# Attention scores from hi and lo parts, and a first modulation with eight tiles

## The chip, the cores and the metric

The kernel runs on one core of a Trainium2 chip. The metric is device time in microseconds (us) for one execution, the median of several. TensorE (PE) multiplies, with weight loads shown as PEld; VectorE (DVE), ScalarE (ACT) and GpSimd (POOL) work elementwise; transfers between HBM and the core's memory are handed out by the queues of SyncE (SP), ScalarE and GpSimd and run on 16 shared DMA engines. Each engine runs its instructions in order.

## The reference

Two layers of a transformer over 256 image tokens x and 256 context tokens, width 1024. In each layer both streams are modulated by rows made of `silu(c) @ w_ada + b_ada`, projected by `w_in` (queries, keys, values, convolution input, gates), mixed by a differential attention and a convolution of 31 taps, and sent through a mixture of 16 experts. In the second layer only x is carried on. The part that the change touches:

```python
hx = modulate(x, mod_x[0], mod_x[1])          # x * (1 + scale) + shift
px = hx @ w_in_l
qx = apply_rope(qk_heads(px[..., :Q_END]), cos, sin)      # 4 heads, 2 maps of 64
s = jnp.einsum('bqhmd,bkhmd->bhmqk', q, k) * (DA_HEAD_DIM ** -0.5)
a = jax.nn.softmax(s, axis=-1)
a = a[:, :, 0] - lam * a[:, :, 1]
return jnp.einsum('bhqk,bkhe->bqhe', a, v)
```

All data is fp32.

## The kernel before

**Products in parts.** The large products of a mixer run in fp32r, a form of fp32 with fewer bits that TensorE takes in one pass. Each operand is split into a hi part (ScalarE casts it to fp32r, L286) and a lo part (the rest, one subtraction, L287), and `mm3` adds three products, hi x hi (L317), hi x lo (L320) and lo x hi (L321), in one bank. `split_unit` does this for a raw weight tile of 128x2048 in two halves; the engine that subtracts is an argument, VectorE by default. The parts lie in rings `whi` and `wlo` of four tiles each. Raw weight tiles lie in `raw`, a ring of three (1 MB each); `load_raw` takes the next one and issues the load on SP's queue (L270). Smaller products run on fp32 data directly, TensorE making several passes; the profile shows such a product as two records.

**The start.** x and ctx are loaded by ScalarE's queue and transposed on TensorE into `xT` (eight blocks, tiles m1a and m1b). `ada(0, 0, "mm")` makes the first modulation: eight raw tiles of `w_ada`, each with four fp32 products of 32 rows (L377), a row out of the bank (L382), transposes, and `modT` (L390, L391). A tile pool named `start` is closed behind it, so the mixer's pool reuses its memory.

**The mixer** (one for each layer). In the first layer `first_block(0)` loads the weights of the first projection block (two raw tiles, 1024x512) and splits them with GpSimd as the subtracting engine; then `modulate` makes, for each of eight k, `hh` on ScalarE (L515) and, on VectorE, the full product (L516) and `hl` (L519). Blocks of projections follow, each 96 products of 512 columns for both streams: two of the convolution, queries, keys, values, and six more for gates. In the second layer the first block is split by VectorE at the end of the layer before.

Queries and keys come out with tokens as rows. On the tiles of x `rope` turns them on VectorE (L621 to L626; its swapped copy `sw` is a "qt" tile), others are copied; TensorE transposes them into the only bank "tr", and ScalarE copies the bank into `kT` (L647) and, scaled, into `qT` (L649), both fp32.

**Attention.** For each tile of 128 queries, four heads and two maps, one score product (L665) of 64 rows, with the two maps in the upper and lower half of TensorE's rows, 512 keys wide for x and 256 for ctx (first layer only). VectorE takes the maximum (L670), ScalarE the exponential (L672), VectorE joins the two maps, TensorE transposes, and the product with the values follows (L686). Between them `pace` and notes of order (`follow`) spread the gates' products and the convolution's taps (L719, L721 on VectorE), so that TensorE has other work while a head's chain runs. The tile's output goes through `o` (a "qt" tile) into hi and lo parts `ah` and `al` (L708).

**End of the convolution.** Four channel blocks: ScalarE and VectorE make z and t (L768 to L770, "zt" tiles, a ring of two) and split z into `ch` and `cl`.

Tiles of one name are a ring: "qt" has three, "at" six (exponentials and transposed maps), "zt" two. The order of instructions within each engine is made when the kernel is built, by a planner that goes by priority in program order and by its own costs and due times.

Of the kernel before, what the change touches and what calls it, by code (L numbers as in the profile page):

```python
# [25 lines left out]
F32 = mybir.dt.float32  # L26
F32R = mybir.dt.float32r
# [133 lines left out]
def dit_kernel(ctx: ExitStack, tc: tile.TileContext, A, out):  # L161
# [40 lines left out]

    ident = C("ident")

    crow = cst.tile([16, 128], F32, name="crow")
    S.dma_start(crow[0:8, :], A["c"].rearrange("o (k p) -> (o k) p", p=128))
    S.dma_start(crow[8:16, :], A["c_ctx"].rearrange("(k p) -> k p", p=128))

# [98 lines left out]
    def block_parts(rs, engs=(V, V)):  # L307

        res = []
        for raw in rs:  # L310
            for hi, lo in split_unit(raw, engs):
                for j in range(2):
                    res.append((hi[:, j * 512:(j + 1) * 512], lo[:, j * 512:(j + 1) * 512]))
        return res
# [24 lines left out]
    G.dma_start(wr[:, :, :NE], A["w_router"].rearrange("(k p) e -> p k e", p=128))  # L339
    br = cst.tile([128, NE], F32, name="br")  # L340
    G.dma_start(br, bcast_rows(A["b_router"]))

    start = scoped("start", tr=2, mm=1)
    st0 = start.open()


    cs = cst.tile([128, KC, 32], F32, name="cs")
# [142 lines left out]
        V.tensor_scalar(dst, r, mean, rs, op0=OP.subtract, op1=OP.mult)  # L490

    def first_block(l):
        return block_parts(block_raws(A["w_in"][l].rearrange("(k p) n -> p k n", p=128), U_OFF + CC, KC), (V, V) if l else (G, G))

    def mixer(l, src, gT, bT, fill, front=None, first=None):

# [79 lines left out]
        if front:  # L576
            front(0, pa, modulate)
        else:
            first = first_block(l)
            for k in range(KC):  # L580
                modulate(k, (0, 1), lambda s: src[k][:, 256 * s:256 * s + 256])

# [17 lines left out]
        if front:  # L600
            front(1, pa, modulate)

            ts = [pa.tile([128, 2, D], F32, name=name) for name in ("ah", "al")]
            for i, name in enumerate(("ln2_g", "ln2_b")):
                rows = xres[i * 128:i * 128 + 128, :]
                G.dma_start(ts[i][:, 0, :], rows)
                G.dma_start(ts[i][:, 1, :], bcast_rows(A[name][l - 1]))
            for i, t in enumerate(ts):
                V.tensor_tensor(t[:, 0, :], t[:, 0, :], ts[0][:, 1, :], op=OP.mult)
                V.tensor_tensor(t[:, 0, :], t[:, 0, :], ts[1][:, 1, :], op=OP.add)  # L610
                G.dma_start(xres[i * 128:i * 128 + 128, :], t[:, 0, :])


        def rope(dst, ps, tt):
            cs_ = C("cos").rearrange("p (t d) -> p t d", t=2)[:, tt, :]
            sn_ = C("sin").rearrange("p (t d) -> p t d", t=2)[:, tt, :].rearrange("p (i two) -> p i two", two=2)
            sw = pa.tile([128, 512], F32, name="qt", bufs=3)
            dv = dst.rearrange("p (h i two) -> p h i two", h=8, two=2)
            pv = ps.rearrange("p (h i two) -> p h i two", h=8, two=2)
            sv = sw.rearrange("p (h i two) -> p h i two", h=8, two=2)  # L620
            V.tensor_tensor(dst.rearrange("p (h d) -> p h d", h=8), ps.rearrange("p (h d) -> p h d", h=8),  # L621
                            cs_[:, None, :].to_broadcast([128, 8, 64]), op=OP.mult)
            for b in range(2):
                V.tensor_tensor(sv[:, :, :, b], pv[:, :, :, 1 - b],
                                sn_[:, None, :, b].to_broadcast([128, 8, 32]), op=OP.mult)
            V.tensor_tensor(dst, dst, sw, op=OP.add)  # L626

        qT = pm.tile([128, NH, 512], F32, name="m0a")
        kT = pm.tile([128, NH, 512], F32, name="m1a")
        vt = pm.tile([128, 4, 512], F32, name="m1b")  # L630
        for which, c0, tiles in (("q", 0, range(nt)), ("k", K_OFF, range(4)), ("v", V_OFF, range(4))):
            for tt, pq in rows_of(c0, tiles):
                if which == "v":
                    S.copy(vt[:, tt, :], pq)
                    continue
                qt = pa.tile([128, 512], F32, name="qt", bufs=3)
                if tt < 2:
                    rope(qt, pq, tt)
                else:
                    S.copy(qt, pq)  # L640
                ps = bank("tr")
                for h in range(NH):
                    transposed(ps[:, h * 128:(h + 1) * 128], qt[:, h * 128:(h + 1) * 128])
                pv = ps.rearrange("p (h n) -> p h n", h=NH)
                sl = slice(tt * 128, tt * 128 + 128)
                if which == "k":
                    S.copy(kT[:, :, sl], pv)  # L647
                else:
                    S.activation(qT[:, :, sl], pv, AF.Copy, scale=0.125)  # L649


        ah = pa.tile([128, NH, 512], F32R, name="ah")
        al = pa.tile([128, NH, 512], F32R, name="al")
        for tt in range(nt):
            k0, nk = (0, 4) if tt < 2 else (2, 2)
            n = nk * 128
# [2 lines left out]
            for h in range(NH):  # L659
                mx = small.tile([128, 2], F32, name="mx")  # L660
                am = []
                for m in range(2):
                    pS = bank("sc")
                    ms = slice(64 * m, 64 * m + 64)
                    hold["pe"] = PE.matmul(pS[:, :n], qT[ms, h, tt * 128:(tt + 1) * 128],  # L665
                                           kT[ms, h, k0 * 128:(k0 + nk) * 128], start=True, stop=True,
                                           tile_position=(64 * m, 0))
                    if m:
                        marks.append(hold["pe"])
                    V.tensor_reduce(mx[:, m:m + 1], pS[:, :n], axis=AX.X, op=OP.max, negate=True)  # L670
                    a = pa.tile([128, 512], F32, name="at", bufs=6)
                    S.activation(a[:, :n], pS[:, :n], AF.Exp, bias=mx[:, m:m + 1], accum_out=sm[:, h, m:m + 1])  # L672
                    am.append(a[:, :n])
# [15 lines left out]

            ss = small.tile([128, NH], F32, name="ss")  # L690
            r0 = small.tile([128, NH], F32, name="r0")
            o = pa.tile([128, 512], F32, name="qt", bufs=3)
            V.reciprocal(r0, sm[:, :, 0])
            for h in range(NH):
                sl = slice(h * 128, (h + 1) * 128)
# [66 lines left out]
        for cb in range(4):  # L762
            ps = bank("mm")
            for tt in range(nt):
                transposed(ps[:, tt * 128:(tt + 1) * 128], acc[:, cb, tt * 128:(tt + 1) * 128])
            z = pa.tile([128, 512], F32, name="zt", bufs=2)
            t = pa.tile([128, 512], F32, name="zt", bufs=2)
            S.activation(z[:, :T], ps[:, :T], AF.Identity, scale=pt[:, 4 + cb:5 + cb], bias=pt[:, 8 + cb:9 + cb])  # L768
            S.activation(t[:, :T], z[:, :T], AF.Tanh)
            V.scalar_tensor_tensor(z[:, :T], t[:, :T], 1.0, z[:, :T], op0=OP.add, op1=OP.mult)  # L770
            split(ch[:, cb, :T], cl[:, cb, :T], z[:, :T])
# [817 lines left out]
    for k in range(KC):  # L1589
# [1 line left out]
        for tt in range(4):  # L1591
            transposed(ps[:, tt * 128:(tt + 1) * 128], xin[tt][:, k * 128:(k + 1) * 128])
        S.copy(xT[k], ps)
    run(ada(0, 0, "mm"))
    start.close()

    def res0(tt):
# [9 lines left out]
    def fill():  # L1607
# [2 lines left out]
        run(steps, 2 if t > 1 else 0)  # L1610

    m = mixer(0, xT, lambda k, s: modT[0][:, k % 4, 2 + k // 4, s:s + 1],
              lambda k, s: modT[0][:, k % 4, k // 4, s:s + 1], fill)
    def experts(l, m, res_src):
        pre_cm = scoped(f"pre{l}", True)
        pre = (pre_cm.open(), N2[l])
# [53 lines left out]
```

## Time and profile before

| | us |
|---|---|
| median of 3 runs | 1266.42 (1264.55 to 1267.15) |
| profiled execution | 1264.6 |
| its span, first to last instruction | 1262.8 |
| TensorE busy in the span | 1110.4 (88%) |
| VectorE busy | 747.4 (59%) |

All durations come from the profiled execution. Its mean granted TensorE clock was 0.946 of full speed; two levels occur, 1.2 and 2.4 GHz. The kernel is read best by stages: the start up to about 40 us, the first mixer to about 380, its output projection and routing to about 460, the first experts to about 715, then the second mixer to about 980 and the second experts to the end.

### The profile page before, as it was taken

The numbers are of one execution on the slowest core, as the hardware profiler recorded it, in microseconds if no ns is written. First come the engines' busy times: TensorE is split into PE (matmuls) and PEld (weight loads), VectorE is DVE, ScalarE is ACT, GpSimd is POOL, SyncE is SP. The second block draws the span as 40 slices with busy tenths as digits, with TensorE's granted clock in tenths as the row PEclk, the third lists the DMA queues.
The fourth block names the chain that finished last, engine by engine and source line by source line (L and its number), as shares of the span: only waits on it lengthen the run. The fifth ranks groups of instructions, "written<-read, shape, count | busy, mean of one in ns | idle before, by whom it ended". The sixth has DMA issues, their size and how long they took to land. (4 is left out here: it accounts for less than half of the span.)

```text
span 1262.8 us, 19232 instructions
## 1 busy us (share of the span) xinstructions
PE 1110.4 (88%) x7412; PEld 809.5 (64%) x7412; DVE 747.4 (59%) x1302; ACT 451.9 (36%) x767; POOL 217.3 (17%) x295
## 2 busy tenths in 40 slices
PE   4699999999999869999998568999999888997991
PEld 1476776676878536766666346767888565765860
DVE  0627987766474733446555389987658752333355
ACT  1422223435341503345454233233654712223240
POOL 2500010000000276110000121101000573010001
PEclk8899999997999979999999778999999989998996
DMA  8666662121239799999999688566327679999993
GB/s 293 226 204 207 236 227 69 34 67 34 67 117 342 309 369 342 388 414 413 417 407 418 258 312 300 207 228 235 102 101 276 236 266 360 415 414 418 398 411 117
DMA packets 81326, 336.32 MB, mean 266 GB/s; under 512 B 10270, under 2 KB 10574, under 8 KB 53328
## 3 DMA queue, kind: packets, MB, share of 16 engines
q1 hardware_dynamic: 67072, 303.06, 62.8%
q0 software_dynamic: 10528, 21.11, 5.0%
q10 hardware_dynamic: 3632, 10.90, 2.3%
q8 instruction: 59, 0.97, 0.3%
q14 instruction: 35, 0.29, 0.1%
HBM read 325.89 MB, written 17.31 MB: 272 GB/s over the span
## 5 line engine op out<-in xcount | busy, mean ns | idle before, releaser
L287 DVE TENSOR_TENSOR wlo<-raw,whi 128x1024 fp32r<-128x1024 f32 x196 | 237.4, 1232 | 95.5 <-ACT whi L286 91.9
L286 ACT CAST whi<-raw 128x1024 fp32r<-128x1024 f32 x204 | 209.5, 1050 | 190.2 <-PE mm L321 84.3
L721 DVE SCALAR_TENSOR_TENSOR cv<-cv,cwt,cv 128x512 f32<-128x512 f32 (+1 forms) x240 | 135.9, 615 | 0.7
L317 PE MATMUL mm<-hh,whi 128*128 128x512 f32 (+1 forms) x384 | 131.1, 349 | 4.6 <-ACT hh L515 4.0
L320 PE MATMUL mm<-hl,whi 128*128 128x512 f32 (+1 forms) x384 | 129.8, 342 | 1.9 <-DVE hl L519 1.8
L321 PE MATMUL mm<-hh,wlo 128*128 128x512 f32 (+1 forms) x384 | 128.8, 343 | 0.0
L317 PEld LDWEIGHTS mm<-hh,whi 128*128 128x128 f32 x384 | 72.8, 191 | 22.5 <-issue 6.5
L321 PEld LDWEIGHTS mm<-hh,wlo 128*128 128x128 f32 x384 | 72.3, 191 | 17.3 <-issue 8.8
L320 PEld LDWEIGHTS mm<-hl,whi 128*128 128x128 f32 x384 | 73.2, 191 | 14.9 <-issue 5.4
L320 PE MATMUL mm<-wlo,xt 128*128 128x512 f32 x192 | 78.5, 409 | 1.3 <-DVE wlo L287 1.3
L317 PE MATMUL mm<-whi,xt 128*128 128x512 f32 x192 | 75.8, 404 | 3.7 <-ACT whi L286 3.7
L321 PE MATMUL mm<-whi,xt 128*128 128x512 f32 x192 | 76.7, 400 | 0.0
L320 PE MATMUL mm<-wlo,hh 128*128 128x512 f32 x176 | 70.0, 398 | 0.0
L317 PE MATMUL mm<-whi,hh 128*128 128x512 f32 x176 | 69.9, 404 | 0.0
L321 PE MATMUL mm<-whi,hl 128*128 128x512 f32 x176 | 69.4, 395 | 0.0
L1070 POOL DMA_INDIRECT ydr<-y,idx x20 | 20.6, 1029 | 186.5 <-DVE y L1368 96.4
L320 PEld LDWEIGHTS mm<-wlo,xt 128*128 128x128 f32 x192 | 36.9, 192 | 16.6 <-DVE wlo L287 5.9
L317 PEld LDWEIGHTS mm<-whi,xt 128*128 128x128 f32 x192 | 37.0, 194 | 13.5 <-ACT whi L286 5.5
L317 PEld LDWEIGHTS mm<-whi,hh 128*128 128x128 f32 x176 | 33.3, 190 | 17.3 <-issue 9.2
L320 PE MATMUL sc<-wlo,at 128*128 128x512 f32 x96 | 40.2, 419 | 2.7 <-DVE wlo L287 2.6
L321 PEld LDWEIGHTS mm<-whi,xt 128*128 128x128 f32 x192 | 37.0, 193 | 7.2
L670 DVE TENSOR_REDUCE mx<-sc 128x1 f32<-128x512 f32 (+1 forms) x48 | 28.4, 598 | 21.4 <-PE sc L665 21.3
(404 smaller groups left out, 2164.0 us busy)
## 6 DMA issues: line engine op xcount, KB each, us to landing
raw<-in_w_ada_dram SPq DMA_DIRECT2D x48, 1024.0 KB
raw<-in_w_e_down_dram SPq DMA_DIRECT2D x47, 1024.0 KB
raw<-in_w_e_up_dram SPq DMA_DIRECT2D x44, 1024.0 KB
raw<-in_w_e_gate_dram SPq DMA_DIRECT2D x41, 1024.0 KB
raw<-in_w_in_dram SPq DMA_DIRECT2D x36, 1024.0 KB
m0a<-in_w_e_up_dram SPq DMA_DIRECT2D x10, 1024.0 KB
raw<-in_w_out_dram SPq DMA_DIRECT2D x8, 1024.0 KB
m0b<-in_w_e_gate_dram SPq DMA_DIRECT2D x8, 1024.0 KB
```

The costliest lines, as they stand in the source:

```text
L286: j = S.copy(hi, src)
L287: i = eng.tensor_tensor(lo, src, hi.bitcast(F32), op=OP.subtract)
L317: i = PE.matmul(ps, lhs[0], rhs[0], start=first, stop=False)
L320: PE.matmul(ps, lhs[0], rhs[1], start=False, stop=False)
L321: PE.matmul(ps, lhs[1], rhs[0], start=False, stop=last)
L670: V.tensor_reduce(mx[:, m:m + 1], pS[:, :n], axis=AX.X, op=OP.max, negate=True)
L721: i = V.scalar_tensor_tensor(av, win, cwt[:, cb, j:j + 1], av, op0=OP.mult, op1=OP.add)
L1070: i = G.indirect_dma_start(out=view, in_offset=None, oob_is_err=False, **kw)
```

## The change

Scores are made of three fp32r products. `qT` and `kT` become fp32r tiles (hi parts); VectorE makes the lo parts `al` (queries, scaled) and `kl` (keys) out of the transpose bank. `al` is the tile that later takes the attention output's lo part, now taken earlier; `kl` is new. Rope's `sw` and the convolution's z and t become "at" tiles, "qt" has two. The first modulation loads into eight tiles of its own in the `start` pool (which also takes `crow`); five steps of it are traced, then the first block's loads and splits, with VectorE subtracting, then the rest.

```diff
     def first_block(l):
-        return block_parts(block_raws(...), (V, V) if l else (G, G))
+        return block_parts(block_raws(...))
...
-            first = first_block(l)
             for k in range(KC):
                 modulate(k, (0, 1), lambda s: src[k][:, 256 * s:256 * s + 256])
...
-            ts = [pa.tile([128, 2, D], F32, name=name) for name in ("ah", "al")]
+            ts = [pa.tile([128, 2, D], F32, name=name) for name in ("ah", "kl")]
...
-            sw = pa.tile([128, 512], F32, name="qt", bufs=3)
+            sw = pa.tile([128, 512], F32, name="at", bufs=6)
...
-        qT = pm.tile([128, NH, 512], F32, name="m0a")
-        kT = pm.tile([128, NH, 512], F32, name="m1a")
+        qT = pm.tile([128, NH, 512], F32R, name="m0a")
+        kT = pm.tile([128, NH, 512], F32R, name="m1a")
+        kl = pa.tile([128, NH, 512], F32R, name="kl")
+        al = pa.tile([128, NH, 512], F32R, name="al")
...
-                qt = pa.tile([128, 512], F32, name="qt", bufs=3)
+                qt = pa.tile([128, 512], F32, name="qt", bufs=2)
...
                     S.copy(kT[:, :, sl], pv)
+                    V.tensor_tensor(kl[:, :, sl], pv, kT[:, :, sl].bitcast(F32), op=OP.subtract)
                 else:
                     S.activation(qT[:, :, sl], pv, AF.Copy, scale=0.125)
+                    V.scalar_tensor_tensor(al[:, :, sl], pv, 0.125, qT[:, :, sl].bitcast(F32), op0=OP.mult, op1=OP.subtract)
...
-                    hold["pe"] = PE.matmul(pS[:, :n], qT[ms, h, tt * 128:(tt + 1) * 128],
-                                           kT[ms, h, k0 * 128:(k0 + nk) * 128], start=True, stop=True,
-                                           tile_position=(64 * m, 0))
+                    qs, ks = slice(tt * 128, tt * 128 + 128), slice(k0 * 128, (k0 + nk) * 128)
+                    for i, (a, b) in enumerate(((qT, kT), (qT, kl), (al, kT))):
+                        hold["pe"] = PE.matmul(pS[:, :n], a[ms, h, qs], b[ms, h, ks], start=i == 0, stop=i == 2,
+                                               tile_position=(64 * m, 0))
...
-            z = pa.tile([128, 512], F32, name="zt", bufs=2)
-            t = pa.tile([128, 512], F32, name="zt", bufs=2)
+            z = pa.tile([128, 512], F32, name="at", bufs=6)
+            t = pa.tile([128, 512], F32, name="at", bufs=6)
...
-    run(ada(0, 0, "mm"))
+
+    raws["from"] = (st0.tile([128, 2048], F32, name=f"first{i}") for i in range(KC))
+    steps = ada(0, 0, "mm")
+    run(steps, KC - 3)
+    from_, raws["from"] = raws["from"], None
+    first = first_block(0)
+    raws["from"] = from_
+    run(steps)
+    raws["from"] = None
     start.close()
```

## Rows read from the trace of the kernel before

**Rows 1.** The page: span, and the clock granted in 40 slices.

```profile
span 1262.8 us, 19232 instructions
...
PEclk8899999997999979999999778999999989998996
```

**Rows 2.** Windows: stretch, length, busy us (instructions) by engine, clock, DMA share, GB/s.

```profile
0.00:24.00 24.00, 5.98 (x31) 1.53 (x31) 1.80 (x8) 1.50 (x2) 9.27 (x17) 0.97 0.94 336
24.00:38.00 14.00, 10.19 (x62) 4.75 (x66) 0.00 (x0) 4.40 (x8) 0.00 (x0) 0.80 0.67 239
...
40.00:50.00 10.00, 6.00 (x16) 4.44 (x15) 6.20 (x11) 8.44 (x16) 6.09 (x4) 0.50 0.63 214
50.00:60.00 10.00, 8.17 (x36) 6.44 (x35) 9.58 (x13) 4.29 (x6) 7.28 (x7) 1.00 0.47 163
60.00:200.00 140.00, 140.00 (x671) 99.15 (x671) 99.90 (x152) 35.00 (x48) 11.80 (x21) 1.00 0.58 200
...
290.00:308.00 18.00, 15.89 (x53) 10.28 (x54) 10.96 (x27) 10.83 (x29) 2.22 (x3) 0.62 0.10 37
...
500.00:700.00 200.00, 186.24 (x1305) 133.27 (x1304) 104.93 (x112) 94.87 (x130) 21.11 (x18) 0.98 1.01 410
...
785.00:910.00 125.00, 125.00 (x710) 91.64 (x709) 100.51 (x197) 45.30 (x80) 9.10 (x15) 1.00 0.54 189
```

**Rows 3.** Timeline of the start: start us, us, engine line op, idle before it.

```profile
0.74 32.38 SPq L270 DMA_DIRECT2D raw<-in_w_ada_dram  x8
...
33.65 14.58 SPq L270 DMA_DIRECT2D raw<-in_w_in_dram  x4
...
37.68 1.07 PE L377 MATMUL mm<-raw,cs 128*32 128x512 f32 x8 [2.51 <-DMA raw<-in_w_ada_dram]
...
41.00 0.73 DVE L516 TENSOR_SCALAR gt<-m1a,modT 128x256 f32<-128x256 f32 x2
41.56 1.99 ACT L286 CAST whi<-raw 128x1024 fp32r<-128x1024 f32 x2 [9.21 <-DMA raw<-in_w_in_dram]
...
43.46 4.04 ACT L515 ACTIVATE hh<-m1a,modT 128x256 fp32r<-128x256 f32 x8
...
44.60 2.07 PE L317 MATMUL mm<-hh,whi 128*128 128x512 f32 x4 [4.00 <-ACT hh L515]
...
51.90 4.89 DVE L516 TENSOR_SCALAR gt<-m1b,modT 128x256 f32<-128x256 f32 x2
...
57.64 0.50 PE L320 MATMUL mm<-hl,whi 128*128 128x512 f32 x1 [1.83 <-DVE hl L519]
...
70.94 0.39 PE L321 MATMUL mm<-hh,wlo 128*128 128x512 f32 x1
```

**Rows 4.** Timeline of TensorE in the first mixer: scores (L665) between plain products.

```profile
182.19 1.13 PE L665 MATMUL sc<-m1a,m0a 64*128 64x512 f32 x4
...
202.51 0.39 PE L321 MATMUL mm<-hh,wlo 128*128 128x512 f32 x1
...
203.65 0.39 PE L320 MATMUL mm<-hl,whi 128*128 128x512 f32 x1
203.97 1.12 PE L665 MATMUL sc<-m1a,m0a 64*128 64x512 f32 x2
205.02 0.50 PE L321 MATMUL mm<-hh,wlo 128*128 128x512 f32 x1
...
206.84 0.40 PE L320 MATMUL mm<-hl,whi 128*128 128x512 f32 x1
```

**Rows 5.** Single lines: count, duration min/median/max in ns, first and last start, forms.

```profile
L665 PE MATMUL sc<-m1a,m0a x96: 376/589/793, 182.2 to 918.6; 64*128 64x512 f32 x64, 64*128 64x256 f32 x32
...
L708 DVE SCALAR_TENSOR_TENSOR al<-tr,pt,ah x6: 743/748/751, 240.4 to 934.2; 128x512 fp32r<-128x512 f32 x6
```

**Rows 6.** Timelines of ScalarE and VectorE at the end of the first convolution.

```profile
294.82 0.78 ACT L768 ACTIVATE zt<-mm,pt 128x512 f32<-128x512 f32 x1 [1.98 <-PE mm L324]
...
301.44 0.68 DVE L287 TENSOR_TENSOR cv<-zt,cv 128x512 fp32r<-128x512 f32 x1
```

More of the change, by code (lines that the diff above doesn't have):

```diff
@@ L203, in dit_kernel @@
     ident = C("ident")
-    crow = cst.tile([16, 128], F32, name="crow")
+    start = scoped("start", tr=2, mm=1)
+    st0 = start.open()
+    crow = st0.tile([16, 128], F32, name="crow")
     S.dma_start(crow[0:8, :], A["c"].rearrange("o (k p) -> (o k) p", p=128))
@@ L341, in dit_kernel @@
     G.dma_start(br, bcast_rows(A["b_router"]))
-    start = scoped("start", tr=2, mm=1)
-    st0 = start.open()
     cs = cst.tile([128, KC, 32], F32, name="cs")
@@ L492, in first_block @@
     def first_block(l):
-        return block_parts(block_raws(A["w_in"][l].rearrange("(k p) n -> p k n", p=128), U_OFF + CC, KC), (V, V) if l else (G, G))
+        return block_parts(block_raws(A["w_in"][l].rearrange("(k p) n -> p k n", p=128), U_OFF + CC, KC))
     def mixer(l, src, gT, bT, fill, front=None, first=None):
@@ L647, in mixer @@
                     S.copy(kT[:, :, sl], pv)
+                    V.tensor_tensor(kl[:, :, sl], pv, kT[:, :, sl].bitcast(F32), op=OP.subtract)
                 else:
                     S.activation(qT[:, :, sl], pv, AF.Copy, scale=0.125)
+                    V.scalar_tensor_tensor(al[:, :, sl], pv, 0.125, qT[:, :, sl].bitcast(F32), op0=OP.mult, op1=OP.subtract)
         ah = pa.tile([128, NH, 512], F32R, name="ah")
-        al = pa.tile([128, NH, 512], F32R, name="al")
         for tt in range(nt):
@@ L691, in mixer @@
             r0 = small.tile([128, NH], F32, name="r0")
-            o = pa.tile([128, 512], F32, name="qt", bufs=3)
+            o = pa.tile([128, 512], F32, name="qt", bufs=2)
             V.reciprocal(r0, sm[:, :, 0])
@@ L1612, in dit_kernel @@
     m = mixer(0, xT, lambda k, s: modT[0][:, k % 4, 2 + k // 4, s:s + 1],
-              lambda k, s: modT[0][:, k % 4, k // 4, s:s + 1], fill)
+              lambda k, s: modT[0][:, k % 4, k // 4, s:s + 1], fill, first=first)
     def experts(l, m, res_src):
```

## The prediction

> **What bounds the kernel now.** I read the page first, for the span and for the line of granted clock [rows 1], then busy time by stage [rows 2]; the reader should see three kinds of stage. Up to about 40 us TensorE mostly waits while the first weights load: the transfers move 336 GB/s up to 24 us and only 239 GB/s from 24 to 38 us, though 410 GB/s flow when nothing holds them back (500 to 700 us) [rows 2]. From 60 to 200 us and from 785 to 910 us, the two mixers, TensorE is busy all the time. From 500 to 700 us, the experts, transfers run at 410 GB/s and are the bound. What shortens a mixer moves everything behind it, because the loads of the experts hang on ring tiles that the mixer frees. The change touches the first kind of stage and the second. Then I read the timeline of the start [rows 3], the scores in the stream of TensorE [rows 4], the groups by line of what is removed and added [rows 5], and the end of the first convolution [rows 6].
>
> **The start.** The eight tiles of the first modulation share a ring of three, so the eight loads are handed out over 32.38 us, and the loads of the first block begin only behind them, at 33.65 us; the last modulation tile reaches TensorE at 37.68 us [rows 3]. With eight tiles no load waits. What must land before the modulation ends is then 8 tiles of 1.05 MB, 2.1 MB of x and ctx, 0.4 MB of constants, 0.1 MB of small things, and two tiles of the first block that are now issued ahead of the last three: 13.1 MB. Up to 24 us 24 x 336 GB/s = 8.1 MB had moved; the other 5.0 MB at 410 GB/s take 12.2 us [rows 2], so the last tile lands at 36.2 us, 1.5 us earlier. From that landing to the first modulate was 41.00 - 37.68 = 3.3 us. Then ScalarE first had to cast the first weights, which had just landed (41.56), and came to hh at 43.46 us; TensorE began 1.14 us later, at 44.60 us [rows 3]. After the change cast and subtraction of those weights are done under the loading, so TensorE begins at 36.2 + 3.3 + 1.14 = 40.6 us.
>
> Then come the 96 products of the first block. Before, they ended at 70.94 + 0.23 = 71.2 us. The granted clock was 0.50, the lower level of 1.2 GHz, from 40 to 50 us, and 1.00 (2.4 GHz) from 50 to 60 us [rows 2]: 5.4 us at the low level from the first product on, in which TensorE made 12 products (16 records less 4 transposes). I let it make the same 12 in 5.4 us; the other 84 at 0.228 us (the five from 202.51 to 203.65 us have that pitch [rows 4]) take 19.2 us, so the block ends at 65.2 us: a gain of **6.0 us**. The wait for hl at 57.64 us goes with it: VectorE's pair of L516 took 4.89 us beside GpSimd's subtraction [rows 3], and GpSimd no longer subtracts. VectorE then needs 0.73 us for each pair of L516 [rows 3] and, by an estimate from that, as much for the subtraction of L519 over the same elements: 1.5 us for each of the eight k, 12 us in all. It ends at 51.5 us, before the first half of the block needs its last part. What is next late is TensorE itself. Bounds: 2.2 us if the first product still comes at 44.60 and only the low-clock products and the wait improve; 9 us if the clock is high from the first product. The four subtractions that VectorE takes over cost about 5 us in a stretch where it is idle (1.80 us busy up to 24 us, none from 24 to 38 us) [rows 2]. The memset of the padded tile now waits until the modulation tiles are read; behind it on GpSimd's queue stand the parameter loads, needed from block two on, some 25 us later: nothing.
>
> **The scores.** There are 48, each recorded as two products in fp32, 32 of them 512 wide (16 in each mixer) and 16 of 256 in the first [rows 5]. A single one costs the stream this: from the plain product at 203.65 to the one at 206.84 us are 3.19 us, holding two scores and three plain products; less 3 x 0.228 that is 2.51 us, or **1.25 us** a score, of which 1.05 is its own [rows 4]. Two that stand side by side, in the two halves of the rows, take the time of one (1.13 us for four records at 182.19). Of the 16 wide ones in either mixer 12 are single and 4 make two pairs, as I count the timeline.
>
> After: three fp32r products of 512 columns, 3 x 0.228 = 0.68 us, and up to 0.20 for going in and out of the half-row tile (1.25 less 1.05). I take 0.80, since part of the 0.20 belongs to fp32. No row shows an fp32r product on 64 rows; the nearest is the 128-row stream, in which the weight load (99.15 us for 671 products, 0.148 each) lies beside products and TensorE never waits [rows 2]. The other end is a load that is not hidden, 3 x (0.228 + 0.148) + 0.20 = 1.33 us a score. So 12 singles save 12 x 0.45 = 5.4 us, and two pairs lose 2 x (1.60 - 1.25) = 0.7: 4.7 us in the first mixer and 4.7 us in the second. The 256-wide ones I take at +0.5 us, between half of a wide one's saving (16 x 0.22) and a loss of half a pair's (8 x 0.18). Sum **9.9 us**. All of it is in streams where TensorE never idles, save the last ones of each mixer.
>
> The low parts cost VectorE 8 operations in the first mixer (four q, four k) and 6 in the second, 0.75 us each by the like form of L708 [rows 5]: 6.0 and 4.5 us. VectorE is busy 99.9 of 140 us and 100.5 of 125 us there [rows 2], so 40 and 24 us of idle time cover them; were that cover gone, the convolution's taps queued behind would come later by just these 6.0 and 4.5 us. Each waits for ScalarE's hi part and holds the only transpose bank until it is done; TensorE comes to the next transposes after half a pair of blocks, some 5 us of products later. I charge 1 us for stalls here (0 to 3).
>
> **Renamed tiles.** Rope's swap, z and t now draw from the six "at" tiles instead of rings of their own, "qt" has two instead of three, "kl" takes the place of "al" in the second mixer's residual rows: nothing, unless the ring is short (third rival).
>
> **Sum.** 6.0 + 9.9 - 1 = 15 us off the profiled execution, 1264.6 us (span 1262.8 and 1.8 around it), gives 1249.5. The median of the runs is 1.8 above the profiled one, so I forecast **1251 us**; 1243 to 1259 by the bounds named.
>
> **The rivals.** (1) *The weights of the half-row products aren't hidden.* The Trainium skill says so in "TensorE: Matmul & The Clock Gate", Part 3 (row/col tiling): a weight load overlaps a running matmul only where the row groups differ, and the three parts use the same rows; the trace disagrees for 128 rows, as said, and no run shows 64. "TensorEngine Tiling", Key Properties, adds that changing the tiling mode drains the engine; the 0.20 us in and out of a score agrees with that. As a mechanism here: 1.33 us a single score and 2.66 a pair, that is 12 x 0.08 + 2 x (2.66 - 1.25) = 3.8 us lost in each mixer; the 256-wide ones take 3 x (0.114 + 0.148) + 0.20 = 0.99 us against half of 1.05 and 0.20 = 0.73, so the 6 singles and 5 pairs among them lose 6 x 0.26 + 5 x (1.98 - 0.73) = 7.8 us, of which I take half, since TensorE isn't always the bound there: some 11.5 us lost against 6 gained, **1272 us**. It decides from about 1.1 us a score on, where scores stop paying for the start. This is the case on the other side. Against it speaks the hidden load of every other fp32r product. Chance 0.10.
>
> (2) *The slow stretch at the end of the first attention goes.* From 290 to 308 us the granted clock was 0.62 on average [rows 2], behind a time of short waits; the changed order of work there may keep it at 1.00: 18 x 0.38 = 6.8 us more, **1244 us**. Chance 0.14.
>
> (3) *The ring of six is short.* z of the convolution's norm is held from 294.82 until its subtraction ends, at about 302 us, and t beside it [rows 6]; with three "at" tiles to each head, only one head at a time fits beside a z and a t. Two heads in each mixer would wait up to 7 us; TensorE has gates' products left to fill most of that in the first mixer, fewer in the second, as an estimate half of it. A longer slow stretch goes with it: 8 to 14 us lost, **1262 us**. Chance 0.12.
>
> (4) *The start gains little*, since the first block's tiles stand ahead of the last three modulation tiles: 2.2 us instead of 6.0, **1255 us**, inside my range. Chance 0.10.
>
> **How the numbers follow.** Forecast 0.54, rivals as above. 0.2% is 2.5 us, about what a measurement of this kernel tells from no change: under 1263.9 is faster. Forecast, (2), (4) and most of (3) are: 0.83. Same: part of (3) and a mild form of (1), 0.07. Slower: the rest, 0.10. The range takes in (2), most of (3) and half of (1)'s mild forms: 1239 to 1264.
>
> **What would show it.** TensorE's first product of block one near 40.6 us and its 96th ending near 65 us; loads of the modulation tiles handed out within a few us; no GpSimd subtraction; a single score some 0.8 us in the stream, with weight loads beside the products; 0.75 us for each low part; the first mixer's end some 11 us earlier and the second's another 4 us. The prediction is wrong if scores take over 1.1 us, or TensorE waits for "at" tiles or the transpose bank, or a stretch at the lower clock level appears or vanishes.

## The result, and the profile after

The changed kernel takes **1283.71 us** (median of 4 runs, 1281.16 to 1287.16); the kernel before took 1266.79 us beside it (4 runs). The ratio is 1.0135 (95% interval 1.0104 to 1.0166): about 17 us slower, where the forecast was 1251 us, faster. The profiled execution took 1283.34 us, span 1281.6. The page of the changed kernel, span and granted clock in 40 slices, as in [rows 1]:

```profile
span 1281.6 us, 19341 instructions
...
PEclk9999999995999979999989869999989999998996
```

The slice with the 5 is new; it lies at the end of the first mixer. Windows of the changed kernel, columns as in [rows 2], and one stretch more that covers this slice:

```profile
24.00:38.00 14.00, 8.76 (x39) 4.49 (x40) 4.72 (x4) 6.71 (x9) 0.00 (x0) 1.00 1.03 405
40.00:50.00 10.00, 7.56 (x33) 5.21 (x32) 7.11 (x18) 7.56 (x16) 3.22 (x3) 0.83 0.49 187
60.00:200.00 140.00, 140.00 (x686) 100.71 (x685) 100.05 (x155) 37.70 (x53) 8.12 (x14) 1.00 0.56 197
284.00:322.00 38.00, 24.73 (x95) 18.03 (x96) 18.82 (x47) 17.93 (x56) 3.09 (x4) 0.55 0.07 26
290.00:308.00 18.00, 11.35 (x47) 7.75 (x48) 7.17 (x21) 6.98 (x28) 1.02 (x1) 0.50 0.00 0
500.00:700.00 200.00, 189.78 (x1283) 136.12 (x1281) 103.28 (x112) 93.14 (x128) 24.46 (x22) 0.95 0.99 396
```

The loads of the start do run freely now (405 GB/s from 24 to 38 us, against 239 in [rows 2]), and the first mixer is still full from 60 to 200 us. But from 284 to 322 us TensorE is busy 24.73 of 38 us. The same stretch of the kernel before:

```profile
284.00:322.00 38.00, 35.44 (x144) 24.61 (x143) 25.00 (x55) 19.95 (x51) 2.22 (x3) 0.82 0.09 28
```

So TensorE is busy 10.7 us less there, and the clock that was granted to it fell from 0.82 to 0.55 on average. What the work waits for is in the timeline of the changed kernel (start us, us, engine, line, operation, idle before it): the last heads, then the end of the convolution.

```profile
302.33 0.48 DVE L681 SCALAR_TENSOR_TENSOR at<-at,cf 128x256 f32<-128x256 f32 x1
...
308.93 0.48 DVE L681 SCALAR_TENSOR_TENSOR at<-at,cf 128x256 f32<-128x256 f32 x1
...
310.31 0.37 ACT L687 COPY at<-tr 128x256 f32<-128x256 f32 x1 [1.92 <-PE tr L326]
310.58 0.78 ACT L771 ACTIVATE at<-mm,pt 128x512 f32<-128x512 f32 x1
...
315.83 1.65 PE L319 MATMUL mm<-cv,whi 128*128 128x512 f32 x3 [3.87 <-ACT cv L288]
```

The heads (L681 joins the two maps of one) follow each other every 3.30 us (a third join lies between the two shown) with nothing beside them. The first z (L771) comes at 310.58 us, right behind the last head's copy (L687), where it came at 294.82 us in [rows 6]; the products that need it start at 315.83 us. The second mixer shows the same order: the last join, then z.

```profile
940.92 0.75 DVE L681 SCALAR_TENSOR_TENSOR at<-at,cf 128x512 f32<-128x512 f32 x1
...
943.23 0.57 ACT L771 ACTIVATE at<-mm,pt 128x256 f32<-128x256 f32 x1
```

By stage, from the timelines of the profiled executions. Block one ends at the start of its last hi x hi product; the first mixer is counted from there to the start of VectorE's last product with a gate (L739 before, L742 after). The second is counted from the 56th of the 64 hi x hi products of its two convolution blocks, some 10 us behind the end of its first block (in the kernel before at 766.51 us), to the same product with a gate:

| us | block one ends | first mixer | from it to the start of the second | second mixer | rest |
|---|---|---|---|---|---|
| before | 70.49 | 305.99 | 390.03 | 194.68 | 301.61 |
| after | 66.98 | 318.19 | 399.74 | 197.87 | 298.82 |
| difference | -3.5 | +12.2 | +9.7 | +3.2 | -2.8 |

### The profile page after: what moved, and what is told of

Same layout as the page of the kernel before. It is cut to its first block, busy times and chain, and to the rows that moved or that the text cites. A ratio compares the mean times of both kernels' runs of the same rounds, so it can differ in the third digit from the quotient of the medians.

```text
span 1281.6 us, 19341 instructions
## 1 busy us (share of the span) xinstructions
PE 1116.2 (87%) x7460; PEld 827.6 (65%) x7460; DVE 752.2 (59%) x1320; ACT 451.6 (35%) x767; POOL 202.7 (16%) x291
## 5 line engine op out<-in xcount | busy, mean ns | idle before, releaser
L289 DVE TENSOR_TENSOR wlo<-raw,whi 128x1024 fp32r<-128x1024 f32 x200 | 240.8, 1224 | 125.2 <-ACT whi L288 121.4
L322 PE MATMUL sc<-wlo,at 128*128 128x512 f32 x96 | 43.9, 457 | 2.6 <-DVE wlo L289 2.5
L323 PE MATMUL sc<-whi,at 128*128 128x512 f32 x96 | 42.1, 438 | 0.0
```

The source lines that it names most:

```text
L289: i = eng.tensor_tensor(lo, src, hi.bitcast(F32), op=OP.subtract)
L322: PE.matmul(ps, lhs[0], rhs[1], start=False, stop=False)
L323: PE.matmul(ps, lhs[1], rhs[0], start=False, stop=last)
```

## The experiments

**Theory A:** z and t are drawn from the six tiles of the heads. A ring gives out its tiles in the order in which the program names them, so z gets its first tile from the last heads but cannot pass them, and the products that filled the gaps between heads come behind the heads. **Rival B:** the scores and the low parts cost more than they save. Each time is a median; the kernel before ran beside each one, and the ratio is to that.

| kernel | us | ratio | 95% interval |
|---|---|---|---|
| at_alone | 1286.32 | 1.0147 | 1.0115 to 1.0178 |
| z_apart | 1256.90 | 0.9909 | 0.9883 to 0.9935 |
| z_again | 1256.94 | 0.9919 | 0.9889 to 0.9949 |
| start_alone | 1258.03 | 0.9931 | 0.9907 to 0.9956 |
| scores_z | 1260.84 | 0.9963 | 0.9939 to 0.9987 |
| lo_gone | 1252.95 | 0.9908 | 0.9872 to 0.9944 |
| hi_only | 1252.23 | 0.9913 | 0.9881 to 0.9945 |
| z_apart_start | 1257.11 | 0.9914 | 0.9889 to 0.9939 |
| start_mid | 1264.52 | 1.0001 | 0.9976 to 1.0027 |
| two_banks | 1258.88 | 0.9930 | 0.9906 to 0.9953 |
| first_banks | 1251.81 | 0.9889 | 0.9857 to 0.9920 |
| first_banks_mid | 1253.27 | 0.9886 | 0.9859 to 0.9913 |

The kernel before took 1267.01 us beside the four kernels z_apart, at_alone, start_alone and z_apart_start; 1263.64 beside scores_z, lo_gone, hi_only and start_mid; 1267.85 beside two_banks and z_again; 1267.37 beside the last two. Stages of the profiled executions, as above:

| us | block one ends | first mixer | from it to the start of the second | second mixer |
|---|---|---|---|---|
| at_alone | 68.95 | 321.37 | 392.73 | 198.94 |
| z_apart | 68.17 | 302.99 | 397.05 | 190.95 |
| z_again | 67.79 | 302.98 | 394.04 | 193.44 |
| start_alone | 65.34 | 305.40 | 391.21 | 192.50 |
| scores_z | 72.42 | 301.38 | 393.95 | 189.61 |
| lo_gone | 70.01 | 297.24 | 395.40 | 189.91 |
| hi_only | 67.05 | 297.67 | 394.51 | 191.25 |
| z_apart_start | 69.51 | 302.17 | 394.81 | 189.48 |
| start_mid | 63.66 | 303.01 | 393.50 | 201.87 |
| two_banks | 68.06 | 296.09 | 394.01 | 197.54 |
| first_banks | 66.45 | 295.01 | 394.26 | 189.58 |
| first_banks_mid | 64.50 | 298.14 | 393.00 | 196.34 |

One profiled execution stands for each kernel in this table. z_apart and z_again are the same kernel, and their stages differ by up to 3.0 us, so a smaller difference tells nothing. Both were taken 4 to 5 us over their medians (1261.89 and 1260.98 us), that of first_banks 4 us under its own (1247.82 us).

**at_alone.** The kernel before, with the ring alone:

```diff
-            z = pa.tile([128, 512], F32, name="zt", bufs=2)
-            t = pa.tile([128, 512], F32, name="zt", bufs=2)
+            z = pa.tile([128, 512], F32, name="at", bufs=6)
+            t = pa.tile([128, 512], F32, name="at", bufs=6)
```

> The kernel before, with one edit: z and t of the convolution's end are drawn from the six at tiles that the heads use, and no longer from a ring of their own. Theory A (the ring of six is what made the changed kernel slower): z can only start behind the last heads, so z comes about 14 us later in the first mixer (before it was at 297.6 us) and 8 to 10 us later in the second, and the kernel is slower by 15 to 25 us: 1282 to 1292 us. Rival B (the scores or the low parts cost more than they save): this edit alone costs at most 3 us, 1267 to 1270 us.

It took 1286.32 us, 1.0147 of before: this edit, by itself, is slower by 15 to 23 us. The timeline of at_alone shows the last join, its copy, and z behind it, 21.7 us later than in [rows 6]:

```profile
314.88 0.48 DVE L678 SCALAR_TENSOR_TENSOR at<-at,cf 128x256 f32<-128x256 f32 x1
...
316.26 0.37 ACT L684 COPY at<-tr 128x256 f32<-128x256 f32 x1 [1.93 <-PE tr L324]
316.53 0.78 ACT L768 ACTIVATE at<-mm,pt 128x512 f32<-128x512 f32 x1
```

Its first mixer is 15.4 us longer than before, the second 4.3 us. Theory A holds; B does not explain it, since the scores are those of before.

**z_apart and z_again.** The changed kernel with z and t in memory that is dead by then:

```diff
-            z = pa.tile([128, 512], F32, name="at", bufs=6)
-            t = pa.tile([128, 512], F32, name="at", bufs=6)
+            z, t = (g0[:, i, 256:] if last else vt[:, i, :] for i in (0, 1))
```

> The changed kernel, with one edit: z and t lie in memory that is dead by then (in the first mixer the values' rows of the first 256 keys, in the second the unused half of a gate tile), one set of both as in the kernel before, and no longer in the ring of the heads. Theory A: the time lost at the end of both mixers comes back, z of the first mixer is at or before 297 us, and the kernel takes 1250 to 1264 us. Rival B: it stays within 5 us of the changed kernel, 1278 to 1284 us.

It took 1256.90 us, and again

> The kernel z_apart once more, beside two_banks on the same chip: 0.99 of the kernel before, as it was measured first.

1256.94 us, so some 27 us less than the changed kernel. In z_again's timeline z is at 288.91 us, with heads before and behind it:

```profile
288.91 0.78 ACT L770 ACTIVATE m1b<-mm,pt 128x512 f32<-128x512 f32 x1 [1.37 <-PE mm L326]
```

In z_again's window of the stretch that stood empty TensorE is busy 35.90 of 38 us:

```profile
284.00:322.00 38.00, 35.90 (x153) 27.52 (x152) 23.73 (x56) 18.35 (x49) 2.08 (x3) 0.82 0.16 55
```

The first mixer is 15.2 us shorter than in the changed kernel, the second 4.4 (z_again) to 6.9 us (z_apart).

**start_alone.** The kernel before with the start of the change, and scores and rings as before:

```diff
-        return block_parts(block_raws(...), (V, V) if l else (G, G))
+        return block_parts(block_raws(...))
...
-    run(ada(0, 0, "mm"))
+
+    raws["from"] = (st0.tile([128, 2048], F32, name=f"first{i}") for i in range(KC))
+    steps = ada(0, 0, "mm")
+    run(steps, KC - 3)
...
+    first = first_block(0)
...
```

> The kernel before with the start of the change alone (eight tiles for the first modulation, VectorE splitting the first weights during it); scores and rings as before. From the two traces: the first product of block one stays near 44 us and its 96th comes 3.5 us earlier, so 3.5 us faster, about 1263 us. The step on record said 6.0 us, 1261 us. Rival: the 3.5 us are given back further on, 1266 to 1267 us.

It took 1258.03 us: 0.69% or 8.7 us faster (5.6 to 11.8), nearer the 6.0 us on record than the 3.5 of the two traces. Block one ends 5.2 us earlier; the other few us show in no single stage. The start varies from kernel to kernel: in the seven others with this very start block one ends at 66.5 to 70.0 us, in the three that start as before (before, at_alone, scores_z) at 69.0 to 72.4 us.

**scores_z.** The kernel before with the lines of the change from `ts` to the score products (the diff ahead of the prediction), z and t as in z_apart, the start as before.

> The kernel before with the scores of the change alone (hi and lo parts, three products), z and t in memory that is dead by then, and the start as before. The step on record: 9.9 us saved less 1 us of stalls, about 1258 us. From the comparison of z_apart with start_alone (1.1 us between their medians): the scores gain hardly anything, 1265 to 1266 us. From the lengths of the two mixers in the same two traces (2.4 and 1.6 us shorter): about 1263 us.

It took 1260.84 us, 0.9963 of before: 4.7 us faster (1.6 to 7.7). That is half of the 8.9 us on record. The two mixers are 4.6 and 5.1 us shorter than before, together 9.7 us, about what the sum had; but the stretch between them is 3.9 us longer (393.95 against 390.03 us). In z_apart and z_again the mixers are 3.0 and 1.2 to 3.7 us shorter.

**hi_only.** z_apart with one product for each score:

```diff
-                    for i, (a, b) in enumerate(((qT, kT), (qT, kl), (al, kT))):
+                    for i, (a, b) in enumerate(((qT, kT),)):
...
```

> The kernel z_apart with one product for each score, hi by hi; the two products with low parts are left out, the low parts are still made. In the trace of z_apart the score products occupy TensorE for 17.9 us in the first mixer and 9.4 us in the second; a third of that is left, so TensorE has 18 us less to do. Rival H (TensorE bounds the mixers, as the sum on record has it): 18 us faster, about 1239 us. Theory G (the ends of the mixers go by the heads' chain, and TensorE's saved time turns into idle time or a lower clock): less than half of it, 1248 to 1257 us.

The ratio, 0.9913, is that of z_apart. The score products alone, by window (stretch, length, TensorE busy us, weight loads, clock, DMA share, GB/s): first before, then the changed kernel, then hi_only, each with the first and the second mixer.

```profile
70.00:376.50 306.50, 25.27 (x64) 8.30 (x64) 0.98 0.37 129
766.50:961.20 194.70, 15.73 (x32) 4.14 (x32) 0.98 0.54 192
```

```profile
67.00:385.20 318.20, 18.90 (x96) 11.08 (x96) 0.94 0.35 124
785.00:982.80 197.80, 10.80 (x48) 5.48 (x48) 0.95 0.54 186
```

```profile
67.00:364.80 297.80, 12.30 (x32) 5.26 (x32) 0.97 0.38 132
759.00:950.50 191.50, 6.69 (x16) 2.49 (x16) 0.96 0.55 193
```

The change frees 41.00 - 29.70 = 11.3 us of TensorE's time, a little more than the sum had it; hi_only frees 10.7 us more (I had worked out 18, but a product that stands alone on half the rows takes 18.99 / 48 = 0.40 us, where three take 29.70 / 48 = 0.62). The 144 products of the change take 25.24 us in lo_gone, where more maps stand side by side, so these sums are good to a few us. With hi_only the first mixer is 5.3 us shorter than in z_again, the second between nothing and 2.2 us, and the whole, by the ratios, no faster that could be measured; the intervals leave room for some 5 us.

So neither theory holds as it stands. Rival H's 18 us are not there, but theory G is not what the first mixer shows. Windows over the whole first mixer, columns as in [rows 2]: before, z_again, hi_only.

```profile
70.50:376.50 306.00, 300.08 (x1386) 217.47 (x1384) 212.56 (x358) 105.88 (x210) 15.60 (x23) 0.98 0.37 129
```

```profile
67.80:370.80 303.00, 295.54 (x1419) 222.59 (x1418) 214.79 (x366) 106.11 (x210) 15.51 (x23) 0.97 0.37 130
```

```profile
67.10:364.70 297.60, 288.80 (x1354) 215.41 (x1352) 215.24 (x365) 105.35 (x210) 15.36 (x23) 0.97 0.38 132
```

TensorE is idle for 5.9, 7.5 and 8.8 us only: of the 6.7 us of TensorE's time that hi_only takes out of z_again's first mixer, all but 1.3 shorten it. In the second mixer TensorE is idle for 11.8 of 193.4 us (z_again) and 12.3 of 191.3 (hi_only). Why these us don't show in the whole is open.

**lo_gone.** z_apart without the 14 low parts:

```diff
+        G.memset(kl.bitcast(F32), 0.0)
+        G.memset(al.bitcast(F32), 0.0)
...
-                    V.tensor_tensor(kl[:, :, sl], pv, kT[:, :, sl].bitcast(F32), op=OP.subtract)
...
-                    V.scalar_tensor_tensor(al[:, :, sl], pv, 0.125, qT[:, :, sl].bitcast(F32), op0=OP.mult, op1=OP.subtract)
```

> The kernel z_apart without the low parts of queries and keys: their tiles are set to zero once, so the two low products add nothing, and VectorE's 14 operations out of the transpose bank are left out; the three products of each score stay. Theory E (the low parts hold the only transpose bank and VectorE, so the last keys and with them the heads come later, and that eats what the scores save): the last key copy of the second mixer comes some 6 us earlier, each mixer is 2 to 4 us shorter, 1249 to 1253 us. Rival F (the ends of the mixers go by the chain of the heads, whatever comes before): within 1.5 us of z_apart, 1255 to 1258 us.

The time, 0.9908 of before, does not tell the two apart. The stages do for the first mixer: 5.7 us shorter than in z_apart though nothing but 8 operations of 0.69 us went away on VectorE, which is busy 214.79 of 303 us there (z_again), and two memsets came in on GpSimd; the last key copy comes at 169.7 us instead of 183.8. With the keys earlier the order of the scores is another one: as I count TensorE's timelines, the 16 wide scores of the first mixer make 8 pairs of maps side by side, in z_apart and z_again 5 pairs and 6 singles. A pair takes the stream as long as a single one, 1.08 us (shown below), so three more pairs are, as an estimate, some 3 of the 5.7 us. The second mixer is 1.0 to 3.5 us shorter. The profiled span is 9.3 us under z_again's (1249.9 and 1259.2), but the kernel before was some 4 us faster beside lo_gone as well, and by the ratios nothing is left: for the whole time this run is inconclusive.

**two_banks.** The same question without leaving anything out: the transposes of queries and keys use a second bank, which is empty at that time.

```diff
-                ps = bank("tr")
+                ps = bank("po" if tt % 2 else "tr")
```

> The kernel z_apart with the transposes of queries and keys going by turns through the bank tr and the bank po, which is empty until the heads begin; low parts and scores as in z_apart. Theory E (a low part holds the only transpose bank until VectorE has made it, and this puts the keys and the heads late): the last key copy of the first mixer comes near 170 us instead of 183.8 us, as without low parts, the first mixer is 4 to 6 us shorter, and the kernel is 3 to 6 us faster than z_apart beside it. If it is VectorE's time or the ring of two qt tiles: the last key copy stays after 180 us and the time is that of z_apart.

Timelines of ScalarE, the copies of the four key tiles of the first mixer; first z_again, then two_banks:

```profile
159.64 0.59 ACT L648 CAST m1a<-tr 128x512 fp32r<-128x512 f32 x1 [8.35 <-PE tr L326]
167.89 0.59 ACT L648 CAST m1a<-tr 128x512 fp32r<-128x512 f32 x1 [2.13 <-PE tr L326]
175.63 0.59 ACT L648 CAST m1a<-tr 128x512 fp32r<-128x512 f32 x1 [1.38 <-PE tr L326]
183.38 0.59 ACT L648 CAST m1a<-tr 128x512 fp32r<-128x512 f32 x1 [2.77 <-PE tr L326]
```

```profile
148.94 0.59 ACT L648 CAST m1a<-tr 128x512 fp32r<-128x512 f32 x1
149.83 0.59 ACT L648 CAST m1a<-po 128x512 fp32r<-128x512 f32 x1 [0.31 <-PE po L326]
158.11 0.58 ACT L648 CAST m1a<-tr 128x512 fp32r<-128x512 f32 x1 [5.08 <-PE tr L326]
158.59 0.59 ACT L648 CAST m1a<-po 128x512 fp32r<-128x512 f32 x1
```

With one bank the copies are 7.7 to 8.3 us apart, with two they come in pairs, and the last is 24.8 us earlier. The first mixer is 6.9 us shorter than in z_again, and its 16 wide scores make 8 pairs, as in lo_gone: theory E fits there. But a second bank takes away more than the low parts brought: in the kernel before, which has none, the copies are 5.1 to 6.2 us apart, and the last is at 167.5 us. TensorE is full in either kernel at that time (50.00 of 50 us from 140 to 190 us); it is the order laid down for it that puts the transposes late when one bank must serve both readers. But the second mixer got 4.1 us longer, and the whole stayed at 0.9930.

**first_banks.** So the second bank only in the first mixer:

```diff
+                ps = bank("po" if tt % 2 and not last else "tr")
```

> The kernel z_apart with the second bank for the transposes of queries and keys in the first mixer alone; in the second all go through tr. In two_banks the first mixer was 6.9 us shorter than in z_again and the second 4.1 us longer, and the two gave the same time. If the first mixer's gain is real and only the second mixer's other order ate it: 5 to 8 us faster than z_apart, 0.984 to 0.988 of the kernel before. Rival (what the first mixer gains is lost in the experts behind it, which wait for transfers): 0.990 to 0.993, as z_apart and two_banks.

1251.81 us, 0.9889 (0.9857 to 0.9920): the fastest median of all, under z_again by 5.1 us, with overlapping intervals, and between the two expectations. The second mixer is back at 189.58 us, the first at 295.01. Its stretch at the end of the first mixer is at the higher level of the clock throughout, as in two_banks (1.00, TensorE busy 34.77 us):

```profile
284.00:322.00 38.00, 34.78 (x168) 27.29 (x169) 22.14 (x44) 17.98 (x44) 1.01 (x1) 1.00 0.16 55
```

**z_apart_start, start_mid and first_banks_mid.** Why was the first product at 44.17 us, not at 40.6? In the changed kernel's timeline the casts of the first weights stand on ScalarE ahead of the copies of x out of the transposes (L1596), and wait for their load:

```profile
27.42 1.99 ACT L288 CAST whi<-raw 128x1024 fp32r<-128x1024 f32 x2 [15.85 <-DMA raw<-in_w_in_dram]
...
32.01 1.06 ACT L1596 COPY m1a<-tr 128x512 f32<-128x512 f32 x2
...
40.04 1.06 PE L376 MATMUL mm<-first,cs 128*32 128x512 f32 x8
...
44.17 1.90 PE L319 MATMUL mm<-hh,whi 128*128 128x512 f32 x4 [1.54 <-ACT hh L514]
```

With the copies go TensorE's transposes, and behind those in its order the modulation's last products, at 40.04 us. z_apart_start puts the casts behind the eighth copy:

```diff
         j = S.copy(hi, src)
+        if hold.get("x") is not None:
+            follow(j, hold["x"])
...
-        S.copy(xT[k], ps)
+        hold["x"] = S.copy(xT[k], ps)
...
```

> The kernel z_apart with one more edit: the casts of the first projection weights on ScalarE are ordered behind its last copy of x out of the transposes. Theory C (these casts, waiting for their weights in front of eight copies of x, held up the transposes and with them the modulation): the copies come some 7 us earlier, the first product of block one at 40 to 41.5 us instead of 44.2, and the kernel is 3 to 4 us faster than z_apart. Rival D (the loads set the end of the modulation): the first product stays at 43 us or later and the time changes by less than 1 us.

The copies came 4.6 us earlier than in z_apart and the last modulation tile was multiplied at 38.13 instead of 41.23 us, but then VectorE's subtractions of the first weights, at 39.80 us, stood ahead of the modulation row (43.21 us), and the first product came at 46.67 us. Neither C nor D: a wait on another engine took its place. start_mid puts the casts behind the fifth copy (the edit against z_apart_start):

```diff
-        hold["x"] = S.copy(xT[k], ps)
+        i = S.copy(xT[k], ps)
+        hold["x"] = i if k == 4 else hold.get("x")
```

> The kernel z_apart with the four casts of the first projection weights ordered behind the fifth of the eight copies of x on ScalarE (in z_apart they stand ahead of most copies, in z_apart_start behind the last, where VectorE's subtractions then stood in front of the row of the modulation). If the order on ScalarE and VectorE sets the first product of block one: the copies come some 4 us earlier than in z_apart, the subtractions end before the modulation row, the first product comes at 42 to 43 us, and the kernel takes 1254 to 1256 us. If the loads set it, or the lower clock at that place does: first product 44 us or later, and no change.

The first product came at 42.45 us and block one ended at 63.66 us, 4.5 us before z_apart. Timeline of start_mid:

```profile
38.32 1.07 PE L378 MATMUL mm<-first,cs 128*32 128x512 f32 x8 [0.37 <-DMA first<-in_w_ada_dram]
```

Here the last tile waits for its load, so the loads end at 38.3 us. Yet the kernel took 1.0001 of before. Its second mixer is 201.87 us, 8 to 11 us longer than z_again's and z_apart's; TensorE's order in it is another one, its 16 scores make 3 pairs (5 in z_again), and from 900 to 940 us the granted clock is 0.83, where z_apart_start has 0.96.

first_banks_mid is first_banks with this edit of start_mid.

> The kernel first_banks with the first casts on ScalarE behind the fifth copy of x, as in start_mid, where the first block ended 4.5 us earlier than in z_apart and the second mixer came out 10 us longer in another order. If start and first mixer add up: 0.980 to 0.985 of the kernel before. If the second mixer comes out in the slow order again: 0.988 to 0.994.

0.9886, as first_banks: block one ended 2.0 us earlier, but both mixers came out longer (298.14 and 196.34 us).

## Why the prediction was wrong, step by step

**Renamed tiles: "nothing, unless the ring is short (third rival)".** This step failed, and it alone turned the sign. The ring was held for short, with heads that would wait up to 7 us for z. It was the other way round: z waits for all heads, because their tiles are named first. The price was given as 8 to 14 us; at_alone measures 18.6 us (15 to 23), and putting z apart in the changed kernel gives back about 27. The rows could have told it: in [rows 6] z is at 294.82 us, and VectorE's timeline of the kernel before has the last head's join (L678) at 326.27 us, so z passed heads whose tiles a common ring hands out before its own:

```profile
326.27 0.48 DVE L678 SCALAR_TENSOR_TENSOR at<-at,cf 128x256 f32<-128x256 f32 x1
```

**Second rival, the slow stretch.** It was to vanish; it grew. From 290 to 308 us the granted clock was 0.62 in [rows 2] and is 0.50 now, with TensorE busy 11.35 of 18 us. It vanished in first_banks and two_banks (1.00 from 284 to 322 us), but z_again, where TensorE is busy for longer (35.90 of 38 us against 34.78 and 34.77), has 0.82 there. So work between the heads alone doesn't keep the clock up, and no run shows what does.

**The start.** Right in sign, and wrong about where. The loads run at 405 GB/s, near the 410 assumed, but end near 38.3 us, not 36.2 (start_mid), and the casts held up the copies of x for longer, so the first product came 0.4 us earlier, not 4.0. What was saved lies in block one: 22.8 us from its first product to its last hi x hi product, 25.9 before, since TensorE no longer waits for hl and got the higher clock sooner (0.83 from 40 to 50 us, 0.50 in [rows 2]). The changed kernel's block one ends 3.5 us earlier, against 6.0 predicted, between the bounds; in time the start alone is worth 8.7 us (5.6 to 11.8), of which I can place 5.2.

**The scores on TensorE.** The sum, 9.9 us, was near the 11.3 us freed, but by luck: its errors cancel. A single score costs the stream 1.08 us and not 0.80; two maps side by side cost 1.09 us together and not 1.60, though [rows 4] had shown two in the time of one. At these prices the 12 singles and two pairs counted would save 12 x 0.17 + 2 x 0.16 = 2.4 us in a mixer and not 4.7. What the sum left out is that the order changes: as I count the timelines, the changed kernel has 5 pairs in either mixer. Timeline of TensorE in the changed kernel, one score and a pair between plain products, and the single one's second and third weight load:

```profile
198.20 0.39 PE L322 MATMUL mm<-hl,whi 128*128 128x512 f32 x1
198.51 0.49 PE L669 MATMUL sc<-m1a,m0a 64*128 64x512 f32 x1
198.85 0.39 PE L669 MATMUL sc<-kl,m0a 64*128 64x512 f32 x1
199.08 0.39 PE L669 MATMUL sc<-m1a,al 64*128 64x512 f32 x1
199.41 0.50 PE L323 MATMUL mm<-hh,wlo 128*128 128x512 f32 x1
199.74 0.39 PE L319 MATMUL mm<-hh,whi 128*128 128x512 f32 x1
```

```profile
187.18 0.39 PE L323 MATMUL mm<-hh,wlo 128*128 128x512 f32 x1
187.50 0.50 PE L669 MATMUL sc<-m1a,m0a 64*128 64x512 f32 x2
187.84 0.40 PE L669 MATMUL sc<-kl,m0a 64*128 64x512 f32 x2
188.07 0.40 PE L669 MATMUL sc<-m1a,al 64*128 64x512 f32 x2
188.39 0.50 PE L319 MATMUL mm<-hh,whi 128*128 128x512 f32 x1
188.73 0.40 PE L322 MATMUL mm<-hl,whi 128*128 128x512 f32 x1
```

```profile
198.62 0.19 PEld L669 LDWEIGHTS sc<-kl,m0a 64*128 64x128 f32 x1
198.85 0.18 PEld L669 LDWEIGHTS sc<-m1a,al 64*128 64x128 f32 x1
```

From 198.20 to 199.74 us are 1.54 us with two plain products of 0.23: 1.08 for the score. From 187.18 to 188.73 are 1.55 us with six score products in them. Inside a score the pitch after the first product is 0.23 us, and the loads at 198.62 and 198.85 lie beside the products before theirs: the first rival is out. The Trainium skill ("TensorE: Matmul & The Clock Gate", Part 3) would have a load on the same rows wait for the running product; these rows say otherwise.

**"What shortens a mixer moves everything behind it."** This step failed second. That the scores lie in streams where TensorE hardly idles was right for the first mixer (5.9 of 306 us idle before), and in scores_z the two mixers are 9.7 us shorter. Of these 4.7 (1.6 to 7.7) reach the end: 3.9 us are lost between the mixers, where every kernel with the new scores takes longer than the kernel before, and 1.9 in block one, which this edit does not touch. What takes them between the mixers no run shows.

**"I charge 1 us for stalls here."** Too little. The low parts did fit into VectorE's idle time at 0.69 us each, as costed, and TensorE doesn't stall; but the one bank moved the last keys of the first mixer by some 16 us (167.5 to 183.4 in z_again) and with them the heads, and that mixer is 5.7 us shorter without the low parts (lo_gone). The prediction had the bank's wait; it didn't see that late keys go with another order of the scores, with fewer pairs.

**What stays open.** The three parts taken alone make -8.7, -4.7 and +18.6, which is +5 us, and the change made +17. Most of the difference is that the ring costs more beside the new scores: 1.0135 over 0.9909 to 0.9919 are 27 to 29 us. The first mixer does not show that (15.2 against 15.4 us), the second little (4.4 to 6.9 against 4.3); 3 to 6 us of it lie in the stretch with the experts of the first layer, 399.74 us long against 397.05 and 394.04 in z_apart and z_again, where transfers are the bound (396 GB/s from 500 to 700 us, 410 in [rows 2]). No run told why. Nor is it known why all kernels with the new scores take 393 to 400 us there, and the others 390 to 393. No run took the move of rope's swap copy and the shorter "qt" ring apart from the scores.

## What to carry to other kernels

Before tiles are renamed into a common ring, look in the trace for users that overtake each other: a ring hands out tiles in program order, and whoever is named last comes last, however early its data is ready. A saving in one stage need not reach the end: the new scores made the two mixers 9.7 us shorter and the kernel 4.7, so look at the stretch behind before a sum is carried on. Price an operation as it stands in the new order, not the old one: here more maps came to stand side by side. Where the order is laid down when the kernel is built, a small edit in one stage can reorder another by 4 to 10 us, so compare kernels by stage before a gain or loss is put down to the edit.

## What the runs showed of the hardware

Six fp32r products of two maps, on the upper and the lower 64 rows, take the stream 1.09 us, as much as the three of one map (1.08): the two halves run at the same time even with three sets of weights each. Going over to half-row products and back lengthens two pitches by some 0.1 us each time: 0.31 and 0.34 us about a score's first product, 0.33 and 0.33 us about the first plain one behind it, where products follow every 0.23 us otherwise. And the granted clock stayed high through the same end of the first mixer (1.00 from 284 to 322 us in first_banks) or fell to 0.55 (changed kernel), with TensorE busy 34.78 and 24.73 of 38 us; at 35.90 us it was 0.82 (z_again), so the busy share alone doesn't tell the clock.
